# A matmul with rotary embedding on one core: a block-transposed pair moved from group 14 to group 4, and the last groups' additions cut anew

## The chip, the cores and the metric

The kernel runs on one core of a Trainium2 chip. The metric is device time in microseconds of one execution; the median of three runs of the kernel before is 151.37 us. Engines are named as in the profile: PE (TensorE), DVE (VectorE), ACT (ScalarE), POOL (GpSimd) and SP (SyncE). PE writes its results to PSUM, which here holds eight banks of 512 fp32 columns: six in the tensor `py`, two in `pt`. POOL works on SBUF alone; DVE and ACT move results from PSUM to SBUF.

## What is computed

```python
batch, seq, hidden, n_heads = (16, 512, 768, 12)      # head_dim 64
y = np.matmul(x, weight)                              # fp32 in and out
y1, y2 = halves of each head of y (32 columns each)
out1 = y1 * cos1 - y2 * sin1
out2 = y2 * cos2 + y1 * sin2
out = concatenate([out1, out2])                       # per head
```

A product with a 768 x 768 weight, and behind it a rotation of the two halves of every head. On the chip the rotation is two steps: DVE multiplies each result by a cosine table and by a signed sine table, both products in one instruction with twice as many output columns as input columns ("product" below), and an addition then adds the first product to the second with its halves swapped.

## The kernel before

**Tiles and groups.** A tile is 128 rows of x (one batch, every fourth row), 768 columns wide. Four tiles of four batches make a group, g = 0 to 15; 64 tiles are numbered i = 4g + s. A group's result is 4 x 768 = 3072 columns in the six banks of `py`; a half group (a *pair* of tiles, 1536 columns) uses three banks, so two pairs alternate.

**Getting x transposed.** PE needs x transposed in fp16. An ordinary tile is loaded by SP (`load`, L202), cast by ACT (`cast`, L237), turned by PE in small transposes into the `pt` banks (`turn_rows`, L257; "a turn") and copied to SBUF by ACT. A *block pair* (`BLOCKS`, L138) takes another way: four quarter loads with a rearranged layout (`load_quarter`, L210) and one DVE transpose in 32 x 32 blocks (`turn_pair`, L283), with no work of PE. In an odd group SP loads the quarters and ACT casts them; in an even group POOL's own DMA queue loads and casts (`pool_loads`, L599, called at the end of each step of the main loop for pairs up to 20 tiles ahead, `P_AHEAD`). Before, the second pair of groups 5 to 14 is a block pair.

**Order of work.** Every instruction goes through `Flow.do` (L42), which keeps for each buffer key the semaphore ticks of its writer and readers and puts the waits on the instruction. Engines run their own queues in program order, and the program order is the hand-written main loop (L640 to L675): matmuls up to a point (`both`, L374), `rope` (L395) for each unit whose banks are complete, DVE's block transposes four tiles ahead (`bturns`), PE turns three tiles ahead, stores, ACT's casts, POOL's loads. Up to tile 57 the two halves of PE's rows work on different banks at once (`walk`, L343, and `one`, L357: the matmuls of L361); the last six tiles use the whole array, piece by piece (`mm_piece`, L331: L336).

**Units.** `units(g)` (L302) cuts a group's 3072 columns into units; `rope` issues one product on DVE for each (L413) and one addition (L430). Groups 1 to 13 have units of 512 and 1024 columns, and in nearly all of them (`whole`, L399) one POOL addition covers both of a half group, 1536 columns. From the second half of group 13 on each unit has its own addition. In group 14 the last 1024 columns are two units of 512, of which DVE adds the second, right after the first product of the last group (`between`, L440). The last group, `LAST` = 15, has four units of 512 and four of 256, of which DVE adds the last.

**Where products go.** The products of each half group take one of three places in turn (`HOMES`, L172): two in the buffer `tq`, one in `w_raw`, the buffer that the weights were loaded into (place 6144 and up). A product for `w_raw` also counts as a writer of all six keys of the weights, `wr00` to `wr21` (`W_HOME`, L162 and L408).

**The end.** Stores of the last group go out on SP and ACT in turn (L671 to L683); `f.finish` (L684, L96) makes ACT wait for every store that may be under way, oldest first, and a closing barrier of all engines follows.

Of the kernel before, what the change touches and what calls it, by code (L numbers as in the profile page):

```python
# [16 lines left out]
class Flow:  # L17
# [78 lines left out]
    def finish(self, e, keys):  # L96
        need = {}
        for k in keys:
            for d in (self.wrote, self.readby):
                for s, v in d.get(k, {}).items():  # L100
                    need[s] = max(need.get(s, 0), v)
        for s, v in sorted(self.settle(e, need), key=lambda q: self.order[q[0]]):
            self.eng[e].wait_ge(self.sem(s), v)


# [1 line left out]
def kernel(  # L107
# [11 lines left out]
    f = Flow(nc, tc)  # L119
    do = f.do  # L120
    P = nc.NUM_PARTITIONS

    B, S, H = x.shape
    NH = int(n_heads)
    D = H // NH
    HD = D // 2
# [4 lines left out]
    QB = 4  # L131
# [3 lines left out]
    LAST = NG - 1  # L135


    BLOCKS = {}  # L138
    for g in range(5, 15):
        BLOCKS[g, 1] = "pool" if g % 2 == 0 and g >= 4 else "sp"  # L140

    def sbuf(name, shape, dt):
# [4 lines left out]
    ident = sbuf("ident", [P, P], FP16)  # L147
# [16 lines left out]
    def products(at, n, lo, hi):  # L164

        mem, base, name = (tq_mem, at, "tq") if at < 6144 else (w_flat, at - 6144, "tw")
        keys = {f"{name}{c // 256}" for j in range(2)
                for c in range(base + j * n + lo, base + j * n + hi, 256)}
        v = mem[:, base : base + 2 * n].rearrange("p (j n) -> p j n", j=2)
        return v[:, :, lo:hi], sorted(keys)  # L170

    HOMES0, HOMES, HOMESL = (0, 1024, 3072, 4096), (6144, 0, 3072), (0, 1024, 2048, 3072, 4096, 5120)  # L172
    ov_b = [sbuf(f"ov{i}", [P, QB * H], FP32) for i in range(NOV)]
    py = nc.alloc_psum_tensor("py", [P, 6 * 512], FP32).ap()
# [4 lines left out]
    def ring(name, n, state={}):  # L179
        k = state.get((id(f), name), 0)  # L180
        state[id(f), name] = k + 1
        return k % n

    def copy(e, o, i_):
        return lambda eng: (
            eng.copy(out=o, in_=i_) if e == "act" else eng.tensor_copy(out=o, in_=i_)  # L186
        )
# [113 lines left out]

    def units(g):  # L302
        if g < LAST:
            cut = [2560] if g == LAST - 1 else []
            at = [0, 512, 1536, 2048] + cut + [3072]
            return [(c, z, py[:, c:z], [f"ps{b}" for b in range(c // 512, z // 512)],
                     "dve" if (g, c) == (LAST - 1, 2560) else "pool")
                    for c, z in zip(at, at[1:])]
        u = [(c, c + 512, py[:, c : c + 512], [f"ps{c // 512}"], "pool")
             for c in range(0, 2048, 512)]  # L310
        if g == LAST:
            for k, (home, bank) in enumerate([
                (py[:, 2048:2304], "ps4"), (py[:, 2560:2816], "ps5"),
                (pt_b[0][:, 0:256], "pt0"), (pt_b[1][:, 0:256], "pt1"),
            ]):
                c = 2048 + 256 * k
                u.append((c, c + 256, home, [bank], "pool" if k < 3 else "dve"))
        return u

    def pieces(g, s):  # L320
# [51 lines left out]
    at = [0, LAG]  # L372
# [17 lines left out]

    ov_of = {}

    late, between, tq_of = [], [], [0]

    def rope(g, u):  # L395
        c0, c1, ps, banks, adder = u
        w, r = c1 - c0, g % SB
        nh = w // D
        whole = 0 < g < LAST - 1 and (g, c0 // 1536) != (LAST - 2, 1)  # L399
        if adder == "dve" and g == LAST:  # L400
            k = len(late)
            tq, keys = xs_b[k][:, 0 : 2 * w].rearrange("p (j n) -> p j n", j=2), [f"xs{k}"]
        elif 0 < g < LAST:
            lo = c0 % 1536
            if lo == 0:
                tq_of[0] = HOMES[ring("tq", len(HOMES))]
            tq, keys = products(tq_of[0], 1536, lo, lo + w)
            if tq_of[0] >= 6144:  # L408
                keys = keys + W_HOME
        else:  # L410
            homes = HOMESL if g else HOMES0
            tq, keys = products(homes[ring(f"tq{g}", len(homes))], w, 0, w)
        do("dve", lambda eng: eng.tensor_tensor(  # L413
            out=tq.rearrange("p j (h d) -> p j h d", d=D),
            in0=ps.rearrange("p (h d) -> p h d", d=D)
            .unsqueeze(1).broadcast_to((P, 2, nh, D)),
            in1=csn[:, :, r, :].unsqueeze(2).broadcast_to((P, 2, nh, D)),
            op=MULT), reads=banks + ["csn"], writes=keys)
        if g not in ov_of:
            ov_of[g] = ring("ov", NOV)  # L420
        o = ov_of[g]

        if whole:
            if c0 % 1536 == 0:
                return
            c0, w = c0 - 512, 1536
            tq, keys = products(tq_of[0], 1536, 0, 1536)

        def add():
            do(adder, lambda eng: eng.tensor_tensor(  # L430
                out=ov_b[o][:, ds(c0, w)].rearrange("p (h t d) -> p h t d", t=2, d=HD),
                in0=tq[:, 0].rearrange("p (h t d) -> p h t d", t=2, d=HD),
                in1=tq[:, 1].rearrange("p (h t d) -> p h t d", t=2, d=HD)[:, :, ::-1, :],
                op=ADD), reads=[q for q in keys if q not in W_HOME], writes=[f"ov{o}c{c}" for c in range(c0, c1, 64)])

        if adder == "dve":
            (late if g == LAST else between).append(add)
        else:
            add()
        if g == LAST and c0 == 0:  # L440
            for more in between:
                more()

    def store(g, c0, c1, e):

        o = ov_of[g]
        b, r = where(g * QB)
        s0, s1 = c0 // H, -(-c1 // H)
        dst = out.rearrange("b (p r) h -> r p b h", r=SB)[r, :, b + s0 : b + s1]
        src = ov_b[o].rearrange("p (b h) -> p b h", b=QB)[:, s0:s1]  # L450
        if (c1 - c0) % H:
            dst = dst[:, 0, c0 - s0 * H : c1 - s0 * H]
            src = src[:, 0, c0 - s0 * H : c1 - s0 * H]
        do(e, lambda eng: eng.dma_start(out=dst, in_=src),
           reads=[f"ov{o}c{c}" for c in range(c0, c1, 64)], dma=f"ov{o}_{c0}")
# [127 lines left out]
    def turns(upto, most=NTILE):  # L583
        while state["turn"] < min(upto, NTILE) and most > 0:
            i = state["turn"]
            state["turn"] += 1
            if not is_block(i):
                most -= 1
                (turn_rows if rows_on[0] else turn)(i, "act")

    def bturns(upto):
        while state["bturn"] < len(pairs):
            gh = pairs[state["bturn"]]
            if gh[0] * QB + 2 * gh[1] >= upto:
                return
            turn_pair(gh)
            state["bturn"] += 1
# [42 lines left out]
    for i in range(QB, NTILE):  # L640
        g, s = divmod(i, QB)
        us = units(g)
        done_to = (s + 1) * H
        rows_on[0] = QB <= i <= QB * LAST
        if i < ROWS:
            if s % 2 == 0:
                for r in range(2):
                    lines[r].extend(walk(i // 2, r))
            for n in range(1, 4):
                both((i - QB) * 4608 + n * 1536)  # L650
                if n == (1 if i > QB else 2):
                    turns(i + T_AHEAD, 1)
        if i == ROWS:
            both(NTILE * 4608)
        for n, p in enumerate(pieces(g, s)) if i >= ROWS else ():
            a, z, _, bank = p
            if n == 1 and i < QB * LAST:
                turns(i + T_AHEAD, 1)
            for c in CHUNKS:
                mm_piece(i, p, c, c == CHUNKS[0], c == CHUNKS[-1],  # L660
                         tick=c == CHUNKS[-1])
            for u in us:
                if u[1] == z:
                    rope(g, u)
        bturns(i + B_AHEAD)
        turns(i + 1 + (T_AHEAD if i > QB else 2), 1)
        for q in stores.get(i, ()):
            store(*q)
        casts(i + 1 + (C_AHEAD if i > QB else 4), 1 + i % 2)
        pool_loads(i + P_AHEAD)  # L670
        if g == LAST:  # L671
            if s == 2:
                store(g, 0, H, "sp")
            if s == 3:
                store(g, H, 2 * H, "act")  # L675
    nc.gpsimd.drain()  # L676
    store(LAST, 2 * H, 2048, "sp")
    store(LAST, 2048, 3 * H, "act")
    store(LAST, 3 * H, 3 * H + 256, "sp")
    store(LAST, 3 * H + 256, 3 * H + 512, "act")  # L680
    for add in late:
        add()
    store(LAST, 3 * H + 512, 4 * H, "sp")  # L683
    f.finish("act", [f"ov{o}c{c}" for o in range(NOV) for c in range(0, QB * H, 64)])  # L684


# [33 lines left out]
```

## Time and profile before

| what | value |
|---|---|
| median of three runs (lowest, highest) | 151.37 us (151.19, 151.68) |
| the profiled execution's own time | 151.05 us |
| its span, first to last instruction | 149.2 us |
| mean granted TensorE clock | 0.993 |
| PE / DVE / POOL / ACT busy | 94% / 85% / 82% / 53% |
| last matmul ends | 143.27 us |
| last addition ends (POOL) | 145.84 us |
| last store lands | 147.63 us |

The span is shorter than the time by what lies around the instructions. All stage times below are counted from the span's start. "Busy" of a PE matmul is modelled, so a busy PE is not a PE at its peak; for this kernel the start-to-start spacing of its matmuls is the better measure. A line such as L430 is a line of the kernel; several groups of instructions share it, and the tiles (`ov<-tq`) and shapes tell them apart.

### The profile page before, as it was taken

To read this page: it belongs to the slowest core of one execution; us is meant where nothing else is said; L and a number is where in the kernel's file an instruction comes from. 1 tells how busy PE (TensorE), PEld (TensorE's weight loads), DVE (VectorE), ACT (ScalarE), POOL (GpSimd) and SP (SyncE) were. 2 spreads that over 40 slices of the span, in tenths; PEclk is the share of its full clock that TensorE was granted. 3 is DMA by queue.
4 is the path that set the end of the run, shared out by engine and by line. 5 is a ranking of instruction groups with operands and counts; after the bars stand their busy time and mean duration, and the time that the engine had idled before them with its cause. 6 is when DMAs were issued, how large, how long until landed. Compare 5 with 4: busy or idle time off the path is not lost.

```text
span 149.2 us, 4382 instructions
## 1 busy us (share of the span) xinstructions
PE 140.7 (94%) x1926; PEld 112.3 (75%) x1926; DVE 126.5 (85%) x92; ACT 78.7 (53%) x92; POOL 122.8 (82%) x68
## 2 busy tenths in 40 slices
PE   6969999999999999999999999999999999999940
PEld 2446588888888888888888888888888888856530
DVE  0156997987888898999999998999989998999990
ACT  3552998778777744466262916193355726163000
POOL 1000495999989989999999999999995979999991
PEclk9999999999999999999999999999999999999997
DMA  4999999999999999999999999999999999996773
GB/s 126 399 396 401 401 406 386 246 259 291 283 325 393 356 353 360 354 401 319 351 351 403 336 348 350 382 372 361 365 367 391 372 400 393 396 389 264 277 307 118
DMA packets 27875, 51.28 MB, mean 344 GB/s; under 512 B 7504, under 2 KB 13392, under 8 KB 27856
## 3 DMA queue, kind: packets, MB, share of 16 engines
q1 hardware_dynamic: 14592, 27.92, 54.6%
q10 hardware_dynamic: 7824, 21.11, 36.0%
q0 software_dynamic: 5440, 1.97, 10.7%
q8 instruction: 15, 0.25, 0.6%
q14 instruction: 4, 0.03, 0.1%
HBM read 27.79 MB, written 25.17 MB: 355 GB/s over the span
## 4 chain that ended last, share of the span: by engine, by line
PE 85%; DVE 6%; POOL 3%; issue 2%; POOLq 0%; DVEq 0%; SPq 0%
PE py L361 70%; PE py L336 5%; PE pt L267 4%; PE py L515 4%; POOL ov L430 3%; DVE w_raw L413 2%; DVE tq L413 2%; PE pt L252 2%; DVE ov L430 1%; POOLq L676 0%; DVE xt L186 0%; DVE w_sb L186 0%; DVE tq L458 0%; DVEq L715 0%; SPq L117 0%
## 5 line engine op out<-in xcount | busy, mean ns | idle before, releaser
L430 POOL TENSOR_TENSOR ov<-tq 128x1536 f32<-128x1536 f32 (+3 forms) x31 | 77.5, 2517 | 18.9 <-DVE tq L413 18.8
L361 PE MATMUL py<-w_sb,xt 64*128 64x512 f16 (+1 forms) x864 | 81.4, 323 | 0.0
L413 DVE TENSOR_TENSOR tq<-py,csn 128x1024 f32<-128x1024 f32 (+2 forms) x46 | 74.6, 1655 | 5.2 <-PE py L361 4.8
L361 PEld LDWEIGHTS py<-w_sb,xt 64*128 64x128 f16 x864 | 60.4, 94 | 10.7 <-issue 0.7
L186 ACT COPY xt<-pt 128x768 f16<-128x768 f16 x42 | 33.6, 800 | 49.1 <-PE pt L267 46.6
L186 ACT CAST xc<-xs 128x768 f16<-128x768 f32 x44 | 38.9, 905 | 9.5 <-DMA xs<-in_x_dram 5.4
L361 PE MATMUL py<-w_sb,xp 64*128 64x512 f16 (+1 forms) x432 | 42.6, 323 | 0.0
L413 DVE TENSOR_TENSOR w_raw<-py,csn 128x1024 f32<-128x1024 f32 (+1 forms) x21 | 35.2, 1677 | 3.8 <-PE py L361 3.6
L430 POOL TENSOR_TENSOR ov<-w_raw 128x1536 f32<-128x1536 f32 (+1 forms) x11 | 33.7, 3071 | 3.3 <-DVE w_raw L413 3.1
L361 PEld LDWEIGHTS py<-w_sb,xp 64*128 64x128 f16 x432 | 30.8, 94 | 5.0
L336 PE MATMUL py<-w_sb,xt 128*128 128x256 f16 (+1 forms) x90 | 15.5, 323 | 1.1 <-DVE w_sb L186 1.1
L267 PEld LDWEIGHTS pt<-ident,xc 64*128 64x128 f16 x456 | 14.8, 95 | 1.7 <-ACT xc L186 0.6
L267 PE MATMUL pt<-ident,xc 64*128 64x64 f16 x456 | 14.8, 190 | 0.0
L336 PEld LDWEIGHTS py<-w_sb,xt 128*128 128x128 f16 x90 | 8.4, 98 | 6.2 <-DVE w_sb L186 1.3
L221 POOL DMA_DIRECT2D xh<-in_x_dram x20 | 11.6, 588 | 0.0
L186 ACT CAST xd<-xb 128x1536 f16<-128x1536 f32 x5 | 8.2, 1634 | 0.0
L515 PE MATMUL py<-tq 128*128 128x512 f16 x12 | 5.4, 626 | 1.4 <-DVE tq L458 1.4
L295 DVE STREAM_TRANSPOSE xp<-xh 128x768 f32<-128x768 f32 x5 | 6.2, 1246 | 0.0
L186 DVE COPY xt<-pt 128x768 f16<-128x768 f16 x2 | 1.1, 556 | 5.7 <-PE pt L252 5.7
L186 DVE CAST w_sb<-w_raw 128x768 f16<-128x768 f32 x6 | 3.3, 557 | 2.6 <-DMA w_raw<-in_weight_dram 2.6
L295 DVE STREAM_TRANSPOSE xp<-xd 128x768 f32<-128x768 f32 x5 | 4.8, 969 | 0.0
L515 PEld LDWEIGHTS py<-tq 128*128 128x128 f16 x12 | 1.6, 144 | 3.6 <-issue 2.2
(20 smaller groups left out, 21.2 us busy)
## 6 DMA issues: line engine op xcount, KB each, us to landing
xs<-in_x_dram SPq DMA_DIRECT2D x44, 384.0 KB, 13.2
out_dram<-ov ACTq DMA_DIRECT2D x41, 384.0 KB, 7.3
out_dram<-ov ACTq DMA_DIRECT2D x6, 768.0 KB, 7.0
xb<-in_x_dram SPq DMA_DIRECT2D x20, 192.0 KB, 15.7
out_dram<-ov SPq DMA_DIRECT2D x4, 768.0 KB, 5.0
w_raw<-in_weight_dram SPq DMA_DIRECT2D x6, 384.0 KB, 6.5
xh<-in_x_dram POOLq DMA_DIRECT2D x20, 96.0 KB, 12.3
out_dram<-ov SPq DMA_DIRECT2D x1, 384.0 KB, 2.5
```

The costliest lines, as they stand in the source:

```text
L186: eng.copy(out=o, in_=i_) if e == "act" else eng.tensor_copy(out=o, in_=i_)
L221: do(e, lambda eng: eng.dma_start(out=dst[ts(q, R)], in_=src[r, q]), writes=[f"{name}q{q}"], dma=name)
L252: do("pe", lambda eng: eng.transpose(pt[:, t, h, :], src[:, t, h, :], ident), reads=[f"xc{c}", "ident"], writes=[f"pt{k}"], tick=(t, h) == ...
L267: do("pe", lambda eng: eng.transpose(pts[r][:, t, h, :], src[rows, t, h, :], ident[rows, rows]), reads=[f"xc{c}", "ident"], writes=[f"pt{r ...
L295: do("dve", lambda eng: eng.transpose(out=dst, in_=src), reads=rd, writes=[f"xp{z}"])
L336: do("pe", lambda eng: eng.matmul(ps, get(t, h), w_sb[:, t, h, a - s * H : z - s * H], start=start, stop=stop), reads=[key, f"w{t}{h}"], w ...
L361: do("pe", lambda eng: eng.matmul(py[:, a:z], get(t, h)[rows], w_sb[rows, t, h, a - s * H : z - s * H], start=start, stop=not opens and en ...
L413: do("dve", lambda eng: eng.tensor_tensor(out=tq.rearrange("p j (h d) -> p j h d", d=D), in0=ps.rearrange("p (h d) -> p h d", d=D) .unsque ...
L430: do(adder, lambda eng: eng.tensor_tensor(out=ov_b[o][:, ds(c0, w)].rearrange("p (h t d) -> p h t d", t=2, d=HD), in0=tq[:, 0].rearrange(" ...
L515: do("pe", lambda eng: eng.matmul(py[:, ts(b, 512)], cold[:, 0:P], cold, start=True, stop=warmed[0] < WARM - 6), reads=["tq0"], writes=[f" ...
```

## The change

1. **Block pairs**: the second pair of groups 4 to 13 instead of 5 to 14. Group 4 is even, so POOL loads that pair.
2. **Finer additions**: from the second half of group 12 on (before: of group 13) every unit has its own addition.
3. **Group 14**: six units of 512 columns, all added by POOL; DVE's addition of the last one goes.
4. **Last group**: two units of 512 and eight of 256. Of the units at 1024 and 1280, and of those at 1536 and 1792, the first product is held and POOL adds both in one addition of 512. The unit at 2304 is added on PE: two fp32 matmuls with an identity matrix (`ident32`) sum the two products into bank `ps2`, and ACT copies the sum to the output buffer. The last unit is added by DVE as before, the others by POOL. The units take the eight banks in turn, so the last two use `ps0` and `ps1` a second time.
5. **The fp32 identity** is copied by POOL in the main loop's step i = 8, into columns 3072 to 3199 of `w_raw`; the copy is a writer of the key `wr20`.
6. **Last stores**: the unit at 2048 goes on SP, then (behind the PE and DVE additions) 2304 on ACT, 2816 on SP, 2560 on ACT.
7. **`finish`** waits only for the stores' semaphores, and the waits are listed in another order. Waits end up two to an instruction, first with last and so on inwards, and run from the innermost pair outwards; in the new order the newest store comes out last.

```diff
-        for s, v in sorted(self.settle(e, need), key=lambda q: self.order[q[0]]):
+        need = {s: v for s, v in need.items() if s.startswith("ov")}
+        old = sorted(self.settle(e, need), key=lambda q: -self.order[q[0]])
+        for s, v in old[:1] + old[1::2] + old[2::2][::-1]:
             self.eng[e].wait_ge(self.sem(s), v)
...
-    for g in range(5, 15):
+    for g in range(4, 14):
         BLOCKS[g, 1] = "pool" if g % 2 == 0 and g >= 4 else "sp"
...
+    ident32 = w_flat[:, 3072 : 3072 + P]
...
         if g < LAST:
-            cut = [2560] if g == LAST - 1 else []
-            at = [0, 512, 1536, 2048] + cut + [3072]
-            return [(c, z, py[:, c:z], [f"ps{b}" for b in range(c // 512, z // 512)],
-                     "dve" if (g, c) == (LAST - 1, 2560) else "pool")
+            at = [0, 512, 1536, 2048, 3072] if g < LAST - 1 else range(0, 3073, 512)
+            return [(c, z, py[:, c:z], [f"ps{b}" for b in range(c // 512, z // 512)], "pool")
                     for c, z in zip(at, at[1:])]
-        u = [(c, c + 512, py[:, c : c + 512], [f"ps{c // 512}"], "pool")
-             for c in range(0, 2048, 512)]
...
+        u = [(c, c + 512, py[:, c : c + 512], [f"ps{c // 512}"], "pool") for c in (0, 512)]
+        for k, e in enumerate(("hold", "pool", "hold", "pool", "pool", "pe", "pool", "dve")):
+            b, c = (k + 2) % 8, 1024 + 256 * k
+            home = pt_b[b - 6] if 6 <= b else py[:, ts(b, 512)]
+            u.append((c, c + 256, home[:, 0:256], [f"pt{b - 6}" if 6 <= b else f"ps{b}"], e))
...
-        whole = 0 < g < LAST - 1 and (g, c0 // 1536) != (LAST - 2, 1)
+        whole = 0 < g and (g, c0 // 1536) < (LAST - 3, 1)
...
+        if adder == "hold":
+            return
+        if held:
+            c0, w = c0 - 256, 512
+            tq, keys = products(held.pop(), 512, 0, 512)
...
+        def add_pe():
+            halves = tq[:, 0], tq[:, 1].rearrange("p (h t d) -> p h t d", t=2, d=HD)[:, :, ::-1, :]
+            ps = py[:, 1024 : 1024 + w]
+            for j in range(2):
+                do("pe", lambda eng: eng.matmul(ps, ident32, halves[j], start=j == 0, stop=j == 1),
+                   reads=keys + ["ident32"], writes=["ps2"], tick=j == 1)
+            do("act", copy("act", ov_b[o][:, ds(c0, w)], ps), reads=["ps2"],
+               writes=[f"ov{o}c{c}" for c in range(c0, c1, 64)])
...
+        if i == 2 * QB:
+            do("pool", lambda eng: eng.tensor_copy(out=ident32, in_=ident),
+               reads=["ident"], writes=["ident32", "wr20"])
...
     store(LAST, 2 * H, 2048, "sp")
-    store(LAST, 2048, 3 * H, "act")
-    store(LAST, 3 * H, 3 * H + 256, "sp")
+    store(LAST, 2048, 3 * H, "sp")
+    for add in after_all + late:
+        add()
+    store(LAST, 3 * H, 3 * H + 256, "act")
+    store(LAST, 3 * H + 512, 4 * H, "sp")
     store(LAST, 3 * H + 256, 3 * H + 512, "act")
-    for add in late:
-        add()
-    store(LAST, 3 * H + 512, 4 * H, "sp")
```

More of the change, by code (lines that the diff above doesn't have):

```diff
@@ L303, in units @@
         if g < LAST:
-            cut = [2560] if g == LAST - 1 else []
-            at = [0, 512, 1536, 2048] + cut + [3072]
-            return [(c, z, py[:, c:z], [f"ps{b}" for b in range(c // 512, z // 512)],
-                     "dve" if (g, c) == (LAST - 1, 2560) else "pool")
+            at = [0, 512, 1536, 2048, 3072] if g < LAST - 1 else range(0, 3073, 512)
+            return [(c, z, py[:, c:z], [f"ps{b}" for b in range(c // 512, z // 512)], "pool")
                     for c, z in zip(at, at[1:])]
-        u = [(c, c + 512, py[:, c : c + 512], [f"ps{c // 512}"], "pool")
-             for c in range(0, 2048, 512)]
[L311 to L317, printed above, removed]
+        u = [(c, c + 512, py[:, c : c + 512], [f"ps{c // 512}"], "pool") for c in (0, 512)]
[3 more added lines that the diff above has]
+            u.append((c, c + 256, home[:, 0:256], [f"pt{b - 6}" if 6 <= b else f"ps{b}"], e))
         return u
@@ L391 @@
     ov_of = {}
-    late, between, tq_of = [], [], [0]
+    late, after_all, tq_of, held = [], [], [0], []
     def rope(g, u):
@@ L409, in rope @@
                 keys = keys + W_HOME
+        elif held:
+            tq, keys = products(held[0], 512, 256, 512)
         else:
             homes = HOMESL if g else HOMES0
-            tq, keys = products(homes[ring(f"tq{g}", len(homes))], w, 0, w)
+            home = homes[ring(f"tq{g}", len(homes))]
+            if adder == "hold":
+                held.append(home)
+            tq, keys = products(home, 512, 0, 256) if adder == "hold" else products(home, w, 0, w)
         do("dve", lambda eng: eng.tensor_tensor(
@@ L427, in rope @@
             tq, keys = products(tq_of[0], 1536, 0, 1536)
+        if adder == "hold":
+            return
+        if held:
+            c0, w = c0 - 256, 512
+            tq, keys = products(held.pop(), 512, 0, 512)
         def add():
@@ L434, in add @@
                 op=ADD), reads=[q for q in keys if q not in W_HOME], writes=[f"ov{o}c{c}" for c in range(c0, c1, 64)])
-        if adder == "dve":
-            (late if g == LAST else between).append(add)
+        def add_pe():
[6 more added lines that the diff above has]
+               writes=[f"ov{o}c{c}" for c in range(c0, c1, 64)])
+        if adder == "pe":
+            after_all.append(add_pe)
+        elif adder == "dve":
+            late.append(add)
         else:
             add()
-        if g == LAST and c0 == 0:
-            for more in between:
-                more()
     def store(g, c0, c1, e):
```

## The prediction

> **What bounds the kernel now.** I read the page's first lines, then the busy time by stage, then the end of the chain of waits, then the costs by shape, and last single instructions on POOL, DVE and PE.
>
> ```profile
> span 149.2 us, 4382 instructions
> ...
> PE 140.7 (94%) x1926; PEld 112.3 (75%) x1926; DVE 126.5 (85%) x92; ACT 78.7 (53%) x92; POOL 122.8 (82%) x68
> ```
>
> Three engines are over 80% busy, so shares alone decide nothing. The stages do (columns: stage, its length, busy us and instructions of PE, PEld, DVE, ACT, POOL, clock, DMA share, GB/s):
>
> ```profile
> 16.00:48.00 32.00, 32.00 (x523) 26.52 (x523) 27.22 (x17) 26.13 (x34) 28.75 (x17) 1.00 1.08 329
> 48.00:121.00 73.00, 73.00 (x1079) 62.68 (x1077) 69.36 (x45) 37.14 (x41) 69.15 (x31) 1.00 1.10 364
> 130.00:136.00 6.00, 6.00 (x57) 3.17 (x56) 5.93 (x5) 3.90 (x5) 6.00 (x4) 1.00 0.88 347
> 136.00:142.00 6.00, 6.00 (x52) 3.94 (x51) 6.00 (x7) 0.80 (x1) 5.92 (x5) 1.00 0.70 268
> 142.00:146.00 4.00, 1.27 (x12) 0.89 (x10) 3.15 (x6) 0.00 (x0) 3.83 (x5) 1.00 0.81 309
> ```
>
> From 16 us until its last matmul ends at 143.27, PE has no gap: nothing before that can be gained except by less PE work. What can be gained lies behind it, and there DVE and POOL are both full from 130 us on. The chain of waits ends so (start, us, what):
>
> ```profile
> 137.62 1.05 DVE ov L430
> 138.66 1.14 DVE tq L413
> 139.81 0.07 issue
> 139.88 2.23 POOL ov L430 x2
> 142.11 0.22 issue
> 142.34 1.95 POOL ov L430 x2
> ...
> 144.97 0.87 POOL ov L430
> ```
>
> The reader is to see that the last thing computed is a POOL addition, ending at 145.84. Its store is issued on ACT's queue at 145.87 and lands at 147.63 (1.77 later). DVE's own last addition ends at 145.25; its store leaves SP at 145.37 and lands at 147.28. ACT then runs seven final waits, the last two at 147.65 and 147.73, and the closing barrier starts at 147.81 and takes 1.35. Costs by shape (POOL, then DVE):
>
> ```profile
> L430 POOL TENSOR_TENSOR ov<-tq 128x512 f32<-128x512 f32 x8 | 10.6, 1338 | 14.6 <-DVE tq L413 14.6
> L430 POOL TENSOR_TENSOR ov<-tq 128x1024 f32<-128x1024 f32 x4 | 9.5, 2375 | 1.2 <-DVE tq L413 1.2
> L430 POOL TENSOR_TENSOR ov<-tq 128x256 f32<-128x256 f32 x3 | 2.3, 780 | 0.0
> ```
>
> ```profile
> L430 DVE TENSOR_TENSOR ov<-w_raw 128x512 f32<-128x512 f32 x1 | 1.0, 1049 | 0.0
> ```
>
> Start to start, back to back, a POOL addition takes 3.43 us for 1536 columns, 2.32 for 1024, 1.24 for 512, 0.68 for 256; a DVE multiplication takes 1.14 for 512 and 0.60 for 256 (the last one 0.68).
>
> **The change, part by part.**
>
> *Block pair from group 14 to 4.* A group without a block pair takes PE 8.50 us, one with it 8.15, so one PE turn of a tile costs 0.175. PE runs 0.35 ahead from group 4 to 13 and gives it back when tiles 58 and 59 are turned at about 125.5 and 127.7. PE's last matmul stays at 143.27: worth 0 at PE. DVE loses a 1.25 us transpose at 126.15, just where it falls behind; it gains one in group 3, where it idles 0.5 us at each of two operations per pair. ACT's two more casts and two more copies late (0.9 and 0.8 each) stand beside an idle ACT. SP loads two more tiles late; those it loads last wait 7 to 14 us between landing and cast. The four POOL DMA issues (2.45 us) leave group 9 and stand at about 24.2 us, where POOL idles only until 25.77:
>
> ```profile
> 25.77 3.48 POOL L430 TENSOR_TENSOR ov<-w_raw 128x1536 f32<-128x1536 f32 x1 [1.54 <-DVE w_raw L413]
> 29.17 2.45 POOL L221 DMA_DIRECT2D xh<-in_x_dram  x4
> 31.63 6.89 POOL L430 TENSOR_TENSOR ov<-tq 128x1536 f32<-128x1536 f32 x2
> ```
>
> So these additions come 0.9 later: the first at 26.65, the second DMA set at 30.05, group 1's second addition 32.4 to 35.85. The new data lands in time: the first such set landed 10.1 to 16.7 after each issue, which puts the last quarter at 26.0 + 16.7 = 42.7, and DVE transposes it at about 44.4.
>
> *The fp32 identity.* POOL copies it right behind that addition. The copy marks a key of w_raw, so the next product that DVE puts into w_raw (34.66) waits for it:
>
> ```profile
> 34.66 1.23 DVE L413 TENSOR_TENSOR w_raw<-py,csn 128x1024 f32<-128x1024 f32 x1 [0.54 <-PE py L361]
> 36.14 2.29 DVE L413 TENSOR_TENSOR w_raw<-py,csn 128x2048 f32<-128x2048 f32 x1 [0.26 <-PE py L361]
> ```
>
> No row has such a copy; the nearest are the 0.20 memset and the 0.29 select that build ident, and above them a 256-column addition (0.72). I take 0.3: the copy ends at 36.15 and DVE starts at 36.2, 1.5 late. Behind it stand that unit and the next: 36.2 + 1.14 + 2.29 = 39.65. PE first writes the last of these banks again at 40.13. Hidden, with 0.45 to spare (nothing to spare at 0.72); every microsecond beyond that is a microsecond of PE and of the time. DVE is level again at 43.16.
>
> *POOL's tail.* Before, the (12,1) addition starts at 121.28, after 0.99 of idling. Split, its first 512 start as soon as the one before ends: 1.37 earlier, 0.35 of it PE's lead. Then: two 1536 split into 512 + 1024, 2 x (1.24 + 2.32 - 3.43) = +0.26; one 1024 of group 14 split, +0.16; group 14's last 512, +1.24; the 0.47 by which LAST's first addition (1.74 against 1.27) ran long beside DVE's addition, gone; one 256 gone to PE, -0.68; the 0.22 of idling at 142.11 and 0.18 of the 0.90 last one gone. Sum -1.26: POOL ends at 144.6 instead of 145.84. If the earlier start did not come about, +0.1 instead.
>
> The row first: LAST's 512 addition on POOL took 1.74 while DVE's addition ran 137.62 to 138.67. The Trainium skill (SBUF — State Buffer, two separate sides) says that a DVE operation with two SBUF inputs and a GpSimd one hold their shared port exclusively for the whole instruction. By that, moving the 512 addition off DVE frees POOL by those 0.47; if the 1.74 had another cause, POOL would end at 145.1 and, as below, the time would still hang on the stores.
>
> *DVE's tail.* With transpose and addition gone, DVE has caught up with PE at LAST: its c=512 product starts at 138.15 (PE's piece ends at 138.05), not 138.59. One 512 and seven 256 follow: 138.15 + 1.14 + 7 x 0.60 = 143.49 for the last product, against PE's end at 143.27; + 0.68 + 0.1 + 0.70 (the row of the same last addition) = 144.97, not 145.25. The twelve added 256-column matmuls replace six of 512 at 0.107 against 0.216 start to start: 0.
>
> *One piece added on PE.* Two fp32 matmuls follow PE's last (143.11), then an ACT copy and ACT's store; ACT's second store, POOL's last piece, queues behind that. Each matmul lies between 0.11 (fp16, 256 columns) and 0.63 (the 512-column ones of L515); no row has four-byte operands, so I take L515's start to start, 0.42: end at 144.2. The copy is below the 0.80 of 768 columns and above a third of it; I take 0.45, with 0.1 ahead of it: 144.8. Stores leave at 144.85 and 145.2 (two issues 0.37 apart); the second lands 1.77 later, 147.0. SP's last leaves at 145.1 and lands 1.91 later, also 147.0.
>
> The Trainium skill (FP8 and Floating Point Precision, TensorE Precision Notes) gives true FP32 four passes; by the 0.107 row that would be an estimated 0.43 a matmul and the same sum.
>
> *Final waits.* The order is turned so that the newest store's wait comes last of all; the step from landing to barrier shrinks from 0.18 to about 0.03: -0.15. The filter drops waits that cost nothing.
>
> **Sum:** last landing 147.63 to 147.0, -0.63; waits -0.15; together -0.78. The profiled execution took 151.05 for its span of 149.2; it should show about 148.4. Off the median 151.37: **150.6 us**.
>
> **Rivals.** *The PE addition is late.* At 0.63 a matmul and 0.80 for the copy ACT's stores leave at 145.6 and 145.97, the last lands at 147.74, and the waits' 0.15 is all but used up: 151.3. For it: both stores share one queue; against: the rows near its middle. *POOL's earlier start does not come about:* POOL ends at 145.95, the last store lands at 147.7: 151.3. Against it: DVE's first (12,1) product is done at 118.08, long before. *Slower: POOL holds up DVE through the w_raw key.* Place: the w_raw product at 34.66; it decides from the moment the identity copy ends after about 36.6. Eight POOL DMAs would be under way at 32 us; the trace shows five at most (62.9 to 64.6), without delay. Were POOL held in the second set until the first quarter landed (24.2 + 10.1 = 34.3, not 30.05), the copy would end at 40.4, DVE's pair at 43.9, and PE would stand 3.8: 151.37 - 0.78 + 3.8 = 154.4. Half a microsecond of it leaves no gain, 1.3 makes it clearly slower.
>
> **How the numbers follow.** Forecast 0.62, late PE addition 0.12, POOL without its start 0.08, slower through POOL and DVE 0.18. About 0.3%, 0.45 us, is what can be told from no change: faster 0.62, same 0.20, slower 0.18. The forecast's own range is 150.1 to 150.9: PE's end plus one product, one addition and one store allows little more than 0.9, and the runs spread by 0.25 around their median. Up to 151.9 it takes in both middle rivals and the mild end of the slow one.
>
> **What would show it.** Right: PE without a gap between 34 and 48 us, its last fp16 matmul 143.3; POOL's first DMA near 24.2; no DVE addition but the last; POOL's last addition near 144.6; last landing near 147.0 and the barrier at once behind it. Wrong: DVE waiting for POOL at the w_raw product and PE for DVE behind it; ACT's copy ending after 145.2; POOL's DMA issues longer than 0.74.

## The result, and the profile after

| | before | changed |
|---|---|---|
| median, first series (lowest, highest; runs) | 151.68 (151.19, 152.46; 7) | 150.59 (150.47, 150.94; 7) |
| the profiled execution, time / span | 151.05 / 149.19 | 150.93 / 149.15 |
| matmul stream begins / last fp16 matmul ends | 17.98 / 143.27 | 18.58 / 143.88 |
| length of that stream | 125.29 | 125.31 |
| *tail*: from there to the end of the span | 5.92 | 5.27 |

The ratio is 0.9934, 95% interval 0.9910 to 0.9958; a second series gave 0.9939 (0.9907 to 0.9971). The spans look alike, 149.2 and 149.1, and would mislead. The stream (from the first matmul of group 1) began 0.60 later in the changed kernel's profiled execution. Over all profiles of this study its beginning lies between 17.68 and 18.77, with the start-up code unchanged, which is more than the change is worth. So executions are compared here by parts: the beginning, the stream, the tail. The change made the stream neither longer nor shorter and the tail 0.65 shorter. What lies around the span went from 1.86 to 1.78; in the experiments below it is 1.86 where the block pair alone was moved (e7) and 1.77 to 1.81 in the others, so this small step belongs to the change, but no run separates which part brings it. Together that is 0.73, within the interval of the runs (0.64 to 1.37 us).

The changed kernel's page and its busy time by stage, as before:

```profile
span 149.1 us, 4421 instructions
...
PE 142.0 (95%) x1942; PEld 114.6 (77%) x1942; DVE 125.7 (84%) x94; ACT 78.9 (53%) x93; POOL 123.3 (83%) x72
```

```profile
16.00:48.00 32.00, 32.00 (x497) 26.32 (x497) 27.87 (x17) 23.68 (x30) 30.04 (x20) 1.00 1.12 307
130.00:136.00 6.00, 6.00 (x71) 3.50 (x67) 5.83 (x6) 3.60 (x5) 6.00 (x5) 1.00 0.95 375
136.00:142.00 6.00, 6.00 (x62) 4.79 (x61) 5.27 (x7) 1.21 (x2) 6.00 (x6) 1.00 0.77 300
142.00:146.00 4.00, 2.75 (x22) 2.13 (x19) 3.33 (x6) 0.37 (x1) 3.16 (x4) 1.00 0.77 295
```

PE still has no gap. DVE, busy for 6.00 of the 6.00 us between 136 and 142 before, is now busy for 5.27: it waits for PE again. POOL is as full as it was. The last pieces of the chain of waits:

```profile
137.88 0.78 PE py L333 x6
138.68 1.99 DVE tq L415 x3
141.02 2.27 DVE tq L415 x4
143.41 0.68 DVE tq L415
144.09 0.61 DVE xs L415
144.79 0.65 DVE ov L437
```

Before, DVE and POOL alternated here and the last was POOL's addition. Now one line of DVE products leads from PE's piece to the end. The early part, POOL and then DVE:

```profile
24.84 2.46 POOL L224 DMA_DIRECT2D xh<-in_x_dram  x4
27.32 3.47 POOL L437 TENSOR_TENSOR ov<-w_raw 128x1536 f32<-128x1536 f32 x1
30.73 2.30 POOL L224 DMA_DIRECT2D xh<-in_x_dram  x4
33.04 3.47 POOL L437 TENSOR_TENSOR ov<-tq 128x1536 f32<-128x1536 f32 x1
36.45 0.29 POOL L682 CAST w_raw<-ident 128x128 f32<-128x128 f16 x1
```

```profile
32.40 2.29 DVE L415 TENSOR_TENSOR tq<-py,csn 128x2048 f32<-128x2048 f32 x1 [0.19 <-PE py L358]
36.78 3.55 DVE L415 TENSOR_TENSOR w_raw<-py,csn 128x1024 f32<-128x1024 f32 x2 [2.08 <-POOL w_raw L682]
```

DVE waits 2.08 for POOL's copy of the identity, as the prediction's working has it, and PE does not notice: the second of these products ends at 40.33, and PE first writes its banks at 40.71. Three lines of the tail, with the addition on PE, DVE's last addition and ACT's copy:

```profile
143.72 1.03 PE L447 MATMUL py<-tq,w_raw 128*128 128x256 f32 x4
144.79 0.65 DVE L437 TENSOR_TENSOR ov<-xs 128x256 f32<-128x256 f32 x1
144.84 0.37 ACT L189 COPY ov<-py 128x256 f32<-128x256 f32 x1 [6.10 <-PE py L447]
```

The four PE records are the two fp32 matmuls: each appears as two records, 0.22 apart. The four span 1.03, and the copy takes 0.37.

### The profile page after: what moved, and what is told of

Same layout as the page of the kernel before. It is cut to its first block, busy times and chain, and to the rows that moved or that the text cites. A ratio compares the mean times of both kernels' runs of the same rounds, so it can differ in the third digit from the quotient of the medians.

```text
span 149.1 us, 4421 instructions
## 1 busy us (share of the span) xinstructions
PE 142.0 (95%) x1942; PEld 114.6 (77%) x1942; DVE 125.7 (84%) x94; ACT 78.9 (53%) x93; POOL 123.3 (83%) x72
## 4 chain that ended last, share of the span: by engine, by line
PE 86%; DMA 5%; DVE 5%; SPq 1%; issue 1%; DVEq 0%
PE py L358 71%; PE py L333 9%; PE pt L270 5%; DMA w_raw<-in_weight_dram 5%; DVE tq L415 3%; SPq L209 1%; PE pt L255 1%; SPq L231 1%; DVE ov L437 0%; DVE xs L415 0%; DVE w_sb L189 0%; SPq L733 0%; DVEq L57 0%; SPq L119 0%
## 5 line engine op out<-in xcount | busy, mean ns | idle before, releaser
L437 POOL TENSOR_TENSOR ov<-tq 128x1536 f32<-128x1536 f32 (+3 forms) x32 | 76.4, 2412 | 18.6 <-DVE tq L415 18.5
L358 PE MATMUL py<-w_sb,xt 64*128 64x512 f16 (+1 forms) x816 | 77.8, 323 | 0.0
L358 PEld LDWEIGHTS py<-w_sb,xt 64*128 64x128 f16 x816 | 58.1, 94 | 9.5 <-DVE tq L415 0.4
L358 PE MATMUL py<-w_sb,xp 64*128 64x512 f16 (+1 forms) x480 | 47.5, 323 | 0.0
L358 PEld LDWEIGHTS py<-w_sb,xp 64*128 64x128 f16 x480 | 34.6, 94 | 5.1
L437 POOL TENSOR_TENSOR ov<-w_raw 128x1536 f32<-128x1536 f32 (+2 forms) x13 | 35.1, 2717 | 2.4 <-DVE w_raw L415 1.8
L333 PE MATMUL py<-w_sb,xt 128*128 128x256 f16 (+1 forms) x126 | 20.1, 309 | 1.4 <-DVE w_sb L189 1.1
L333 PEld LDWEIGHTS py<-w_sb,xt 128*128 128x128 f16 x126 | 11.4, 98 | 7.6 <-DVE w_sb L189 2.8
```

Source lines behind the costliest of these rows:

```text
L333: do("pe", lambda eng: eng.matmul(ps, get(t, h), w_sb[:, t, h, a - s * H : z - s * H], start=start, stop=stop), reads=[key, f"w{t}{h}"], w ...
L358: do("pe", lambda eng: eng.matmul(py[:, a:z], get(t, h)[rows], w_sb[rows, t, h, a - s * H : z - s * H], start=start, stop=not opens and en ...
L437: do(adder, lambda eng: eng.tensor_tensor(out=ov_b[o][:, ds(c0, w)].rearrange("p (h t d) -> p h t d", t=2, d=HD), in0=tq[:, 0].rearrange(" ...
```

## The experiments

All edits are to the changed kernel unless another base is named; each was timed beside the kernel before on its chip. The last five columns are read from the traces. POOL and DVE stand for the end of the engine's last addition, and landing for the arrival of the last store, all three counted from the end of the last fp16 matmul. "Theory" and "rival" below are the two readings that each expectation sets against each other.

| run | time (median) | ratio to before (95%) | stream | POOL | DVE | landing | tail |
|---|---|---|---|---|---|---|---|
| before | | | 125.29 | 2.56 | 1.98 | 4.36 | 5.92 |
| changed | 150.59 | 0.9934 (0.9910-0.9958) | 125.31 | 1.27 | 1.56 | 3.86 | 5.27 |
| e1_block14 | 151.73 | 1.0014 (0.9985-1.0043) | 125.65 | 2.48 | 2.77 | 4.71 | 6.15 |
| e2_no_pe_add | 151.07 | 0.9959 (0.9929-0.9988) | 126.19 | 1.96 | 2.24 | 4.10 | 5.55 |
| e3_coarse | 151.12 | 0.9964 (0.9934-0.9995) | 125.53 | 1.80 | 2.09 | 4.03 | 5.48 |
| e4_old_waits | 150.79 | 0.9959 (0.9932-0.9985) | 125.30 | 1.27 | 1.56 | 3.87 | 5.34 |
| e5_sp_last | 151.01 | 0.9959 (0.9933-0.9985) | 125.30 | 1.26 | 1.55 | 3.77 | 5.17 |
| e6_nine_copies | 153.38 | 1.0099 (1.0059-1.0140) | 127.80 | 1.27 | 1.55 | 3.87 | 5.27 |
| e7_block_only | 151.39 | 0.9993 (0.9965-1.0021) | 125.36 | 2.35 | 1.77 | 4.15 | 5.70 |
| e8_dve_adds14 | 150.78 | 0.9946 (0.9914-0.9978) | 125.30 | 1.30 | 1.59 | 3.90 | 5.31 |
| e9_old_cut | 151.10 | 0.9974 (0.9948-1.0000) | 125.27 | 2.35 | 1.77 | 4.11 | 5.52 |
| e10_two_dve | 150.76 | 0.9928 (0.9900-0.9956) | 125.94 | 0.59 | 1.47 | 3.66 | 5.06 |
| e11_after_again | 150.87 | 0.9939 (0.9907-0.9971) | 125.30 | 1.26 | 1.55 | 3.87 | 5.26 |
| e12_late_loads | 150.48 | 0.9936 (0.9920-0.9953) | 125.30 | 0.58 | 1.47 | 3.66 | 5.06 |

The intervals of the times are some 0.3% wide to either side. They show that e6 is slower than the kernel before and that e1 and e7 are not measurably faster, and little else. The tails repeat to 0.01 (changed, e6 and e11) and carry the finer verdicts, each on one execution. Where the stream is clearly longer than 125.3, that is e6's own effect or gaps of PE, told of at the end; the gaps are not counted as effects of the edits.

### The block pair back in group 14

```diff
-    for g in range(4, 14):
+    for g in range(5, 15):
```

> The changed kernel with the block pair back in group 14 (groups 5 to 14), all else as changed. Measure: the tail, from the end of PE's last fp16 matmul to the end of the span: 5.92 us before, 5.27 changed. Theory (POOL's and DVE's work behind PE decides; the block transpose at 126 us delays the product that POOL's 1024-column addition of group 13 waits for): POOL ends 1.0 to 1.2 later, tail 5.6 to 5.8, time 0.3 to 0.5 above the changed kernel. Rival (the pair's place is neutral, since PE's last matmul stays where it is): tail 5.25 to 5.35, time as changed.

The whole gain goes: the tail is 6.15, longer than before the change (5.92) and than the 5.6 to 5.8 expected, and the ratio is 1.0014, to which a gap of PE of 0.35 (last section) may have added its part. POOL ends 1.21 later, as the theory has it, and the place is the one it names: POOL idles 1.04 ahead of group 13's addition of 1024 columns, 0.19 in the changed kernel:

```profile
130.26 6.09 POOL L437 TENSOR_TENSOR ov<-tq 128x1024 f32<-128x1024 f32 x4 [1.04 <-DVE tq L415]
```

The rest, which the theory did not have, is DVE's:

```profile
142.48 3.86 POOL L437 TENSOR_TENSOR ov<-tq 128x512 f32<-128x512 f32 x4
144.77 1.86 DVE L437 TENSOR_TENSOR ov<-xs 128x256 f32<-128x256 f32 x1
```

DVE's last addition, 0.65 in the changed kernel, took 1.86, from 144.77 to 146.63: it stood until POOL's four additions were through at 146.34. So here a late POOL costs twice, by its own end and by holding DVE. The rival is refuted: without the gap PE's stream is 125.30 as before, so PE does not care where the pair stands, but the tail does.

### Only the block pair moved (base: the kernel before)

```diff
-    for g in range(5, 15):
+    for g in range(4, 14):
```

> The kernel before with only the block pair moved (groups 4 to 13). Theory (POOL still has its idling before the whole addition of group 12, and DVE its addition of group 14's last unit that holds POOL 0.47): POOL ends 0.1 to 0.3 earlier, tail 5.7 to 5.85 against 5.92 before. Rival (the moved transpose is the whole gain): tail 5.3 to 5.4.

Tail 5.70, POOL 0.21 earlier: as the theory has it. The move alone is worth 0.22; its absence from the changed kernel costs 0.88 of tail. So the edits need each other. Without the move (e1) POOL waits 1.04 for DVE and never catches up. Without the finer cut (here) POOL idles 0.98 ahead of group 12's second addition, and its first addition of the last group takes 1.59 instead of 1.27, since DVE's addition of group 14 is under way when it begins.

### Whole additions in groups 12 and 13

```diff
-        whole = 0 < g and (g, c0 // 1536) < (LAST - 3, 1)
+        whole = 0 < g < LAST - 1 and (g, c0 // 1536) != (LAST - 2, 1)
```

> The changed kernel with whole 1536-column additions up to the first half of group 13, as before. Theory: POOL idles about 1.0 again before the addition of group 12's second half, saves 0.26 of splitting, and ends 0.7 to 0.8 later; tail 5.5 to 5.7. Rival (POOL's early start is lost again in later waits for DVE): tail 5.2 to 5.3.

POOL idles 0.98 again where the theory says, but ends only 0.53 later (0.7 to 0.8 expected). The tail is 5.48, just under the theory's 5.5 to 5.7 and far from the rival's: the finer additions are worth 0.21. DVE's last addition stands behind POOL here too (1.18).

### No addition on PE

```diff
-("hold", "pool", "hold", "pool", "pool", "pe", "pool", "dve")
+("hold", "pool", "hold", "pool", "pool", "pool", "pool", "dve")
```

> The changed kernel with the unit at 2304 added by POOL instead of PE. Theory: POOL has 0.68 more and ends that much later behind PE's last matmul; its last store leaves ACT at most 0.3 later than in the changed kernel, where it queued behind the PE piece's store: tail 5.35 to 5.6 against 5.27. Rival (the PE addition costs more than it saves, since ACT's copy holds ACT's queue and the last store): tail 5.0 to 5.25.

POOL ends 0.69 later, and DVE's addition stands behind it as in e1: it takes 1.34 and ends at 2.24 instead of 1.56. The tail is 5.55, so the addition on PE is worth 0.28. The rival, that ACT's copy costs more than POOL saves, is refuted.

### The last group cut as before

```diff
-        u = [... for c in (0, 512)]
-        for k, e in enumerate(("hold", "pool", "hold", "pool", "pool", "pe", "pool", "dve")):
+        u = [... for c in range(0, 2048, 512)]
+        for k, e in enumerate(("pool", "pool", "pool", "dve")):
...
-            b, c = (k + 2) % 8, 1024 + 256 * k
+            b, c = k + 4, 2048 + 256 * k
```

> The changed kernel with the last group cut as before (four units of 512, four of 256, the first seven added by POOL, the last by DVE; no addition on PE), all else as changed. Theory (the cut into 256 as such brings nothing, since DVE catches up with PE either way; only the missing PE addition counts): tail as without the PE addition, 5.45 to 5.65. Rival (the finer cut carries the gain): tail 5.75 to 5.95, the changed kernel's 5.27 being out of reach without it.

Tail 5.52, no worse than the new cut without the PE addition (e2, 5.55): cutting 1024 to 2047 into 256 brings nothing as long as PE adds nothing, and the rival is refuted. But the reason given for it, that DVE catches up either way, is not what happened. With the old cut DVE starts its last addition 0.30 later than in e2 and POOL ends 0.39 later, while DVE's addition gets in after one of POOL's (0.56, against 1.34 in e2) and ends 0.47 earlier. The two cancel. What the finer cut is worth beside the PE addition was not tried.

### Group 14's last unit added by DVE

```diff
-                     ..., "pool")
+                     ..., "dve" if (g, c) == (LAST - 1, 2560) else "pool")
...
+        if g == LAST and c0 == 0:
+            for more in between:
+                more()
```

> The changed kernel with group 14's last unit added by DVE again, behind the last group's first product. Theory: DVE loses about 1.0 there, its product of the unit at 512 starts 0.4 to 0.5 late and the lag stays to its last addition: tail 5.5 to 5.7 against 5.27. Rival (an addition is cheaper on DVE, and POOL is the later one): POOL ends 0.8 earlier, tail 4.9 to 5.2.

Both readings are refuted: the tail is 5.31, 0.04 from the changed kernel.

```profile
138.07 0.68 DVE L439 TENSOR_TENSOR ov<-w_raw 128x512 f32<-128x512 f32 x1
138.29 2.94 POOL L439 TENSOR_TENSOR ov<-tq 128x512 f32<-128x512 f32 x2 [0.79 <-DVE tq L417]
138.66 3.01 DVE L417 TENSOR_TENSOR tq<-py,csn 128x1024 f32<-128x1024 f32 x4
```

DVE's addition takes 0.68, not the 1.05 of before: POOL was at work when it began there and is not here. DVE is free at 138.75 and goes on with the next product at once, about when PE has its bank ready. POOL idles 0.79 in place of the addition. Its last five additions then follow DVE's second product of the last group back to back in both kernels, so what POOL did before no longer matters.

### The final waits in the old order

```diff
-        old = sorted(self.settle(e, need), key=lambda q: -self.order[q[0]])
-        for s, v in old[:1] + old[1::2] + old[2::2][::-1]:
+        old = sorted(self.settle(e, need), key=lambda q: self.order[q[0]])
+        for s, v in old:
```

> The changed kernel with the final waits in the old order. Theory: two waits of about 0.08 each follow the last landing again: tail 5.40 to 5.45 against 5.27, too little for the times to tell. Rival (the newest wait last makes no difference): 5.27.

From the last landing to the end of the span 1.48 instead of 1.40, tail 5.34: one wait of 0.08 behind the last landing, not two. That is half of what was expected, but the effect is there.

### POOL's last store on SP

```diff
-    store(LAST, 3 * H + 512, 4 * H, "sp")
-    store(LAST, 3 * H + 256, 3 * H + 512, "act")
+    store(LAST, 3 * H + 256, 3 * H + 512, "sp")
+    store(LAST, 3 * H + 512, 4 * H, "sp")
```

> The changed kernel with the store of POOL's last piece (2560) moved from ACT, where it queues behind the PE piece's store, to SP, ahead of DVE's last piece. Theory: in the changed kernel this store leaves 0.48 after POOL's end; on SP it leaves 0.05 after it and DVE's follows 0.37 later; the last landing is 0.25 to 0.35 earlier: tail 4.9 to 5.05 against 5.27. Rival (landings crowd each other, so that the last one stays about 2 us behind whatever leaves last): tail 5.15 to 5.3.

Tail 5.17: 0.10, not 0.25 or more. The last issue is now DVE's piece, and DVE ends 1.55 behind PE whatever the queues do; the store leaves at 1.67 and lands 2.10 later. The theory had the times of leaving right; the landing, and with it the tail, are as the rival has them.

### Two DVE additions at the end

```diff
-("hold", "pool", "hold", "pool", "pool", "pe", "pool", "dve")
+("hold", "pool", "hold", "pool", "pool", "pe", "dve", "dve")
```

with both stores on SP, as in the edit above.

> The changed kernel with the last two units (2560 and 2816) both added by DVE, PE's unit as changed, and both stores on SP. POOL then ends with the unit at 2048, 0.6 after PE's last fp16 matmul, and holds the port no more when DVE adds. Theory (DVE's addition of 0.65 is mostly waiting for POOL; alone a 256-column one takes about 0.3): DVE ends 1.4 to 1.5 after PE, the last store leaves at 1.6 and lands at 3.5 to 3.6: tail 4.85 to 5.05 against 5.27. Rival (the additions take their 0.65 each on DVE): DVE ends 2.2 after PE, tail 5.5 to 5.7.

```profile
144.18 1.27 DVE L415 TENSOR_TENSOR xs<-py,csn 128x512 f32<-128x512 f32 x2
145.38 0.75 DVE L437 TENSOR_TENSOR ov<-xs 128x256 f32<-128x256 f32 x2
```

With POOL out of the way two additions take 0.75, little more than one took beside it (0.65). One alone takes 0.41 (about 0.3 was expected), so 0.24 of the 0.65 was waiting: less than half, not most of it. DVE ends at 1.47 and the tail is 5.06, a hair above the theory's range. The rival is refuted.

### The identity copied nine times

```diff
-            do("pool", lambda eng: eng.tensor_copy(out=ident32, in_=ident),
-               reads=["ident"], writes=["ident32", "wr20"])
+            for _ in range(9):
+                do("pool", lambda eng: eng.tensor_copy(out=ident32, in_=ident),
+                   reads=["ident"], writes=["ident32", "wr20"])
```

> The changed kernel with the identity copied nine times in place of once, one behind the other. Theory (the price of the slower rival: DVE's product into w_raw waits for the last copy, and PE for DVE beyond a slack of 0.38): eight more copies of 0.29 to 0.35 put the product 2.3 to 2.8 later, PE stands 1.9 to 2.4 in front of the banks of group 3's second half, and the time rises by that; tail unchanged. Rival (the banks have more room than the last use of them shows): time as changed, PE without a gap.

Its trace, POOL, DVE and PE in turn:

```profile
36.37 3.14 POOL L683 CAST w_raw<-ident 128x128 f32<-128x128 f16 x9
```

```profile
39.54 3.55 DVE L415 TENSOR_TENSOR w_raw<-py,csn 128x1024 f32<-128x1024 f32 x2 [4.89 <-POOL w_raw L683]
```

```profile
43.15 1.68 PE L358 MATMUL py<-w_sb,xt 64*128 64x512 f16 x16 [1.51 <-DVE w_raw L415]
```

Counted from the stream's beginning, the product starts 2.81 later than in the changed kernel, and PE's matmuls in front of its banks stand 1.88 from start to start. The stream is 127.80, and the time is 1.0% above the kernel before, where the changed kernel is 0.7% below. A gap told of in the last section (0.47) is in the stream too, and takes its part of the wait: 2.81 - 0.38 - 0.47 = 1.96, near the 1.88 and near the 2.02 by which the stream is longer beyond that gap. So the slow rival's mechanism is real, and a slack of 0.38 fits as the point where it sets in.

### POOL's block loads two tiles later (base: two DVE additions)

```diff
-    C_AHEAD, T_AHEAD, B_AHEAD, P_AHEAD = 5, 3, 4, 20
+    C_AHEAD, T_AHEAD, B_AHEAD, P_AHEAD = 5, 3, 4, 18
```

> The version with two DVE additions at the end, and POOL's block loads called 18 tiles ahead in place of 20, so that group 6's set stands behind the identity copy. Theory (the copy is late only for the second set of DMA issues ahead of it, 2.30): the copy ends 2.3 earlier, before PE has the w_raw product's banks ready, and DVE waits for nothing there; matmul stream 125.3, tail 5.05, time 0.6 to 1.0 below the kernel before. It also shows whether PE's gap 15.2 after its stream began (0.64 in the version this is made from) stays. Rival (the loads come too late): DVE waits at group 6's block transpose, near 62, and the stream is longer by that.

```profile
33.59 0.30 POOL L682 CAST w_raw<-ident 128x128 f32<-128x128 f16 x1
33.83 2.31 POOL L224 DMA_DIRECT2D xh<-in_x_dram  x4
```

```profile
34.68 1.23 DVE L415 TENSOR_TENSOR w_raw<-py,csn 128x1024 f32<-128x1024 f32 x1 [0.54 <-PE py L358]
```

The copy is done at 33.89, the product waits for PE alone, the last of the second set lands at 52.27 against its use at 60.62: so the second set of DMA issues ahead of the copy was enough to make it late. The tail is 5.06 again and the time 150.48 us: with e10 this is the best version run. That it beats the changed kernel is shown by the tail (0.20), not by the times.

### The changed kernel again

> The changed kernel as it is, beside these two on one chip. Theory: tail 5.25 to 5.30 again and matmul stream 125.3, while the start of the stream moves by some tenths from run to run; time 0.5 to 0.8 below the kernel before. Rival (the tail of the first profile was a lucky one): tail 5.4 or more.

Tail 5.26, stream 125.30, ratio 0.9939; the stream began at 18.77. The first profile's tail was no accident.

## Why the prediction was right, point by point

The direction, the size (0.78 forecast; 0.65 in the tail, 0.73 with what lies around the span) and the path held. That 150.6 met 150.59 almost exactly is partly luck: the forecast set out from 151.37, the median of three runs, and longer series of the kernel before gave 151.5 to 151.7. Step by step, tail times from the last fp16 matmul's end:

- **PE's end stays.** Right: stream 125.29 and 125.31.
- **POOL early and the identity.** Right nearly to the tenth: the copy took 0.29 (0.3 taken), DVE's product started 18.20 after the stream's beginning (18.22), and 0.38 was left of the slack (0.45). POOL's DMA issues took 2.46 and 2.30 with eight DMAs under way, so the slow rival's trigger did not come. The first set's last quarter landed at 41.13 and DVE transposed at 44.88. e6 shows the rival's price, e12 its source. The working reads the room for DVE's new transpose too high: the rows of the kernel before show an idle of 0.47 to 0.54 at the first product of a pair and 0.19 to 0.26 at the second, not 0.5 at each. It cost PE nothing all the same.
- **POOL's end.** 1.33 forecast, 1.27 measured, but the sum that led there had a term too many. The addition moved from DVE to POOL was entered with +1.24 - 0.47. e8 shows that it changes POOL's end by 0.03, since its last additions hang on the product of LAST's second unit and so on PE. That the backlog of additions was done just when this product was, and the sum came out right, is luck. The earlier start itself is real: group 12's second addition starts 1.42 earlier, counted from the stream's beginning (1.37 forecast). But it does not reach POOL's end whole: without it POOL ends 0.53 later (e3), and it is lost if the block pair is back in group 14 (e1).
- **DVE's end.** 1.70 forecast, 1.56 measured. That the transpose's removal lets DVE catch up is right; the addition's removal is not needed for it (e8). The transpose was worth more than the working says: it stood there as 1.25 on DVE and 0 at PE, and its way into the tail, over the wait of POOL for group 13's product, is missing. e1 puts the move at 0.88 of tail.
- **The shared port.** The row of 1.74 was read with the Trainium skill's rule (SBUF — State Buffer, two separate sides). e1 (0.65 grown to 1.86 until POOL's additions were through), e8 (1.05 shrunk to 0.68 with POOL idle) and e10 (two additions in 0.75) agree with it. So do the ends: in all twelve profiles in which DVE's last addition overlaps POOL's, it ends 0.28 to 0.29 after one of them, and POOL's first addition of the last group ends 1.13 after DVE's addition of group 14 in all three kernels that have that one (before, e7, e8). By the rule the engine that starts second waits until the first one's instruction is through; in e1 DVE waited through the rest of one of POOL's additions and two more, in e2 and e3 through the rest of one and one more, while before and in e7 and e9 it got in after one. What decides that is open. The trace does not show the port, so the rule fits the times but is not proved by them.
- **The addition on PE.** Matmuls done at 0.87 (0.93 forecast), copy at 1.33 (1.53). The value taken for a matmul, 0.42, is what two records 0.22 apart make; the estimate from the four passes of the Trainium skill (FP8 and Floating Point Precision, TensorE Precision Notes) was 0.43. e2: worth 0.28.
- **The last landing.** 3.73 forecast, 3.86 measured. The store left earlier than forecast (1.75 against 1.93) and took 2.11 to land instead of 1.77: it was the last of three that left within 0.4 us, unlike the row it was priced by. This term was 0.34 too small; the earlier leaving made up for 0.18 of it, and the rest is why 0.65 and not 0.78 was gained. That the two other stores made it slow fits e5, e10 and e12, but was not tried alone.
- **The waits.** 0.15 forecast. The step from landing to the span's end went from 1.56 to 1.40, and with the old order back (e4) it is 1.48: the order is worth 0.08. The other 0.08 comes with which store lands last: in the kernel before ACT has two wait instructions to run behind the last landing, in e4 one, and in the changed kernel none, since its last wait of all is the one for that landing.

Taken together: of the tail's 0.65, the block pair's place is the condition, and the finer additions (0.21), the PE addition (0.28) and the waits (0.08) are worth something on top of it. DVE's relief of group 14's addition (0.04) and the finer cut without the PE addition (nothing) are not. Differences of less than 0.05 between single profiles are not claimed.

## What to carry to other kernels

Where one engine runs without a gap, compare executions by what comes behind its last instruction; beginnings that wander by a microsecond hide a change of half of one. In the tail, ask of each engine what its last operation hangs on: work taken off an engine that will wait for a later product anyway is worth nothing (e8), while a delay behind which it has no idle moment left comes back in full, and costs more still if its additions then stand in the way of another engine's (e1). Before giving a buffer's spare columns to something new, look at who waits for that buffer's keys, and at what is queued ahead of the new writer (e6, e12).

## What the runs showed of the hardware that was not expected

**A gap of PE that nothing in the kernel waits for.** In e1, e2, e3, e6 and e10 PE pauses 15.2 us after the stream began, in the middle of one tile's transposes, released by no semaphore. In the waits of e2 between 30 and 45 us it reads so (waiting engine, "issue" for nothing the profile shows, total, times, longest):

```profile
PEld pt L270 <- issue: 0.6, 1, 0.6
PEld py L358 <- issue: 0.4, 1, 0.4
```

The first line is this gap. The profile shows the transfers that bring the engines' instructions as a DMA queue of its own, in packets of 16 KB; each time the second of these packets behind the stream's beginning had begun 2.59 to 2.77 before PE went on. The gap is there exactly where that packet began late:

| packet begins, from the stream's beginning | gap |
|---|---|
| 11.60 to 12.53 (before, changed, e4, e5, e7, e8, e9, e11, e12) | none |
| 12.78 and 12.79 (e1, e3) | 0.35, 0.24 |
| 13.01 (e6) | 0.47 |
| 13.14 and 13.23 (e10, e2) | 0.64, 0.62 |

The second line of e2 is another such gap, 23.4 us after the stream began, where PE's matmuls stand 0.31 from start to start. There the third packet had begun 2.80 before PE went on, at 20.86, later than in any other profile; the two gaps together are the 0.89 by which e2's stream is longer. The changed kernel, at 12.53, stands right at the edge, the kernel before at 12.07. That PE waits for its instructions there fits all fourteen profiles but was not tried. What makes the packet late is open: e12, which differs from e10 by the later loads alone, has it 0.71 earlier and no gap, but that is one profile each. What moves the stream's beginning from run to run is open too.

**Small stores.** Of the last stores, of 128 KB each, most took 1.72 to 1.95 from issue to landing, and 2.10 to 2.12 when they were the last of three that left within 0.4 us (changed, e4, e5, e6, e8, e10, e11, e12). Three others were slow as well: 2.04 for the middle one of e5's three, and 2.24 and 2.13 in e1, which left 0.21 and 0.68 behind one of 256 KB.
